# Two-layer decoder trunk: a second ordinary pair in three SwiGLUs, extra operands made later, and layer norm and rotation without GpSimd

## The chip, the cores and the metric

The kernel runs on one core of one Trainium2 chip. The metric is the device time of one execution in microseconds (us); lower is better. All data is 32 bits wide.

## The reference

For 512 tokens of width 1024, two layers run one after the other, and a final RMSNorm follows:

```
x = x + 0.5 * swiglu(rms_norm(x, g1), w_gate, w_up, w_down)     # d_ff = 2816
x = x + mixer(rms_norm(x, g2))
x = x + 0.5 * swiglu(rms_norm(x, g3), w_gate, w_up, w_down)
```

with `swiglu(x) = (silu(x @ w_gate) * (x @ w_up)) @ w_down`. So there are four SwiGLUs, two in each layer.

The mixer of layer 0 (the even one) projects its input to q, k and v of 8 heads of 64 and to the two halves u and v of a gMLP. Attention is block-sparse, which for 512 tokens is plain causal attention over at most two blocks of 256. The gMLP is

```
v = layer_norm(v.reshape(B, S, 8, 64), ln_g, ln_b)       # per group of 64 channels
mixed = einsum('gts,bnsgd->bntgd', tril(w_s), v) + b_s   # chunks of 128 tokens
return u * mixed
```

The mixer of layer 1 (the odd one) is a differential attention: 8 heads, two q/k maps of 64 per head, 128 values per head; the two softmaxes are subtracted with a weight lambda, and each head's output is normalised. In both, q and k are rotated by position in their first 16 of 64 dimensions: `x * cos + swap(x) * sin`.

## The kernel before

Everything stands transposed: `x[k]` for k = 0 to 7 holds 128 features by 512 tokens, in on-chip memory for the whole run. Weights stream from HBM in chunks of 128 x 1024. Each chunk is split into two fp32r parts: ScalarE copies it to `w_hi` (L120), VectorE subtracts to make `w_lo` (L121). A product is then three matmuls (`mm3`, L168 to L170): hi by hi, and the two cross terms. Activations are split in the same way (`xh`, `xl` in `Norm.split`, L217 and L218).

All work is issued as a list of slots (`Stream`). A slot names the chunks it needs and the function that issues its matmuls. `run` walks over the slots: `step()` first issues the side work that was put down for this slot by `later(n, fn)` ("n slots from now"), then the splits of chunks for later slots (four ahead in a SwiGLU, the next slot's in a mixer), then the slot's matmuls. A scheduler then orders each engine's instructions by the dependencies, by that order of issue and by its own estimates; each engine works in the resulting order.

A SwiGLU has 22 tiles of 128 features. Tile 0 and tile 11 are computed as ordinary products (`first`, `gate`, `up`, `product`), gate and up 8 x 3 matmuls with 512 columns each. The other tiles are taken in pairs (s, s + 11), and each pair, gate and up together, is computed by a Strassen-Winograd scheme with seven products instead of eight on halves of the tokens (`Step`, L424 to L426 in the profile: seven slots of 24 matmuls with 256 columns). That scheme needs sums of weights (partly made by a DMA that adds, L369, partly on VectorE, L380) and extra operands, which are sums of parts of x: `SevenNorm.sums_for(p)`, p = 0 to 3 makes them (three small splits and three sums, L281 to L290 and L264: seven operations on VectorE, five on ScalarE, each with 256 columns), and `last_sums` (L300, L301) a last one. The extra operands are made as soon as the x they need exist (`feed`: one slot after the k-th x), and for the first SwiGLU all four two slots after its first one.

The norm's factor for each token comes from squares summed over features (on GpSimd, L311, but for the first), a matmul with ones (`pc`, L240), ten small operations on VectorE (`rsqrt`, L191 to L202, result `rcol`), four transposes (`pr`, L322) and a copy on ScalarE (`R`, L326, also `norm.row`). It multiplies the SwiGLU's products after the matmuls (`product`), so TensorE can begin before it is known.

In the even mixer the gMLP's v is centred (`center`), scaled by its root (L840), multiplied by the gain and given the bias on GpSimd (L842, L843), and split one slot later (`split_gate`). In both mixers `rotated` makes a q or a k: VectorE swaps rows (L638) and multiplies by cosine (L639), GpSimd multiplies the swapped one by sine (L640) and adds the two (L641). Then ScalarE and VectorE split it (`qs`, L653 and L654; `ks`, L661 and L662). The heads' further stages (scores with exponentials `e`, transposes `pt`, their splits `ph` and `pl`, the product `o`) are put down some slots later.

Of the kernel before, what the change touches and what calls it, by code (L numbers as in the profile page):

```python
# [11 lines left out]
F32 = mybir.dt.float32  # L12
# [6 lines left out]
P = 128  # L19
# [13 lines left out]
def trunk_kernel(ctx: ExitStack, tc: tile.TileContext, a, out):  # L33
# [137 lines left out]

    warm = const.tile([P, 1], F32, name="warm")
    nc.vector.memset(warm, 0.0)
# [81 lines left out]
    class SevenNorm(Norm):  # L255
# [57 lines left out]
        def feed(self, k):  # L313
            self.split(k)
            self.square(k)
            if k in KHI:
                st.later(1, lambda: self.sums_for(KHI.index(k)))
# [30 lines left out]
    def ffn(which, norm, feed):  # L348
        gu, wd = a[f"gu{which}"], a[f"wd{which}"]
        H = {}  # L350

# [172 lines left out]
        def first(wg, wu):  # L524
            norm.finish_soon(1 + int(which == 0))
            pg, pu = bank("pg"), bank("pu")
            for ks in [[k] for k in range(KT)] if which == 0 else (range(KT - 1), range(KT - 1, KT)):
                for b, w in ((pg, wg), (pu, wu)):
                    project(b, w, norm, ks)
            for p in range(4):  # L530
                norm.whole(p)
            st.later(2 + int(which == 0), lambda: product(0, pg, pu))

        def gate(f):
# [5 lines left out]
        def up(f):  # L540
            def fn(w):
                b = bank("pu")
                project(b, w, norm)
                st.later(1, lambda: product(f, banks[f], b))
                st.later(1, norm.last_sums)
            return fn

        st.add([chunk(gu[0, 0]), chunk(gu[0, 1])], first, dense=True, raws=6)
        st.add([chunk(gu[HF, 0])], gate(HF), dense=True, raws=6)
        st.add([chunk(gu[HF, 1])], up(HF), dense=True, raws=6)  # L550
        add(1, 1)
        for s0, s1 in PARTS:
            for s in range(max(s0, 1), s1):
                for c in ORDER:
                    if c != 1:
                        add(s, c)
                    elif s + 1 < HF:
                        add(s + 1, 1)
            cols = slice(s0 * P, s1 * P)
            for ds in [(0, 1)] + [(d,) for d in range(2, KT)]:  # L560
                st.add([chunk(wd[0, d][:, cols], wd[1, d][:, cols]) for d in ds], down(ds, s0, s1),
                       dense=True, raws=6)
# [71 lines left out]
    def rotated(pq, tables, place):  # L634

        cr, sr = tables
        sw, q = tmp("sw"), tmp("q")
        nc.vector.stream_shuffle(sw, pq, SWAP)  # L638
        nc.vector.tensor_mul(q, pq, cr)  # L639
        nc.gpsimd.tensor_mul(sw, sw, sr)  # L640
        nc.gpsimd.tensor_add(q, q, sw)  # L641
        st.mids.append(lambda: place(q))
# [139 lines left out]
    def even_mixer(norm, feed):  # L782
# [9 lines left out]
        def begin():  # L792
            norm.finish_soon()
            st.later(3, lambda: box.update(rope=rope_tables(norm)))
            for c in range(2):
# [7 lines left out]
                wsl.append(lo)  # L803
            ln = act.tile([P, 2, T], F32, name="ln", tag="e", bufs=EB)
            for n, name in enumerate(("lng", "lnb")):
                box[name] = ln[:, n]
                nc.sync.dma_start(box[name], a["ln"][n])
            bs = act.tile([P, T], F32, name="bs", tag="e", bufs=EB)
            nc.sync.dma_start(bs, a["bs"])
            box["bs"] = bs.rearrange("p (m t) -> p m t", t=P)  # L810

# [24 lines left out]
        def finish_gate():  # L836
            rsqrt(rs.rearrange("p t g -> p (t g)"), s2.rearrange("p t g -> p (t g)"), 1.0 / 64, TT * 8)
            for t in range(TT):
                g = cen[t]
                nc.vector.tensor_tensor(by_group(g), by_group(g),  # L840
                                        rs[:, t, :, None].to_broadcast([P, 8, 64]), op=OP.mult)
                nc.gpsimd.tensor_mul(g, g, box["lng"])  # L842
                nc.gpsimd.tensor_add(g, g, box["lnb"])  # L843
            st.later(1, lambda: [split_gate(t) for t in range(TT)])

# [20 lines left out]
        def mix_group(m):  # L866
# [3 lines left out]
            for nn in range(2):  # L870
# [7 lines left out]
                for h in range(2):  # L878
                    r = slice(h * 64, h * 64 + 64)
                    nc.vector.tensor_tensor(mixv[r, 2 * nn:2 * nn + 2], bv[r, :, h],  # L880
                                            box["bs"][r, m:m + 1, :].to_broadcast([64, 2, P]), op=OP.add)
            nc.vector.tensor_mul(mix, mix, u[m])
# [56 lines left out]
    def odd_mixer(norm, feed):  # L939
# [71 lines left out]
        def values(p):  # L1011
            def fn(wa, wb):
                b = [bank("pv"), bank("pv")]
                for t in range(TT):
                    r = slice(t * P, (t + 1) * P)
                    for k in range(KT):
                        w = (wa, wb)[k // 4]
                        s = slice((k % 4) * 256, (k % 4 + 1) * 256)
                        mm3(b[t // 2][:, (t % 2) * 256:(t % 2 + 1) * 256], norm.hi[k][:, r], norm.lo[k][:, r],
                            w[0][:, s], w[1][:, s], k == 0, k == KT - 1)  # L1020
                halves = [t2k("h", "v", F32R).rearrange("p (n c) -> p n c", n=2) for _ in range(3)]
# [5 lines left out]
                box["v", p] = (vh, vl, vw)  # L1027
            st.add([chunk(a["ov"][p, 0]), chunk(a["ov"][p, 1])], fn)

# [167 lines left out]
```

## Time and profile before

| | |
|---|---|
| Median of three runs | 1886.41 us (1886.3 to 1890.41) |
| The profiled execution: time, span | 1890.68 us, 1888.9 us |
| Mean granted TensorE clock | 0.986 |
| TensorE (PE), matmul busy | 1834.6 us, 97% of the span |
| VectorE (DVE) busy | 1359.1 us, 72% |
| ScalarE (ACT) busy | 875.4 us, 46% |
| GpSimd (POOL) busy | 415.0 us, 22% |
| Mean HBM traffic | 127 GB/s |

The span is the time from the first to the last instruction; some 1.8 us of the execution lie outside it. The shares are means over stages that differ, so where an engine waits has to be read by stretch. The granted clock is a share of 2.4 GHz: 1.00 is full speed, 0.50 is 1.2 GHz.

### The profile page before, as it was taken

The page shows a single profiled execution, that of the slowest core. Times are in us where ns is not written, and L with a number is a line of the kernel's source. Part 1 is how long each engine was busy: PE and PEld are TensorE (multiplying, and loading weights), DVE is VectorE, ACT ScalarE, POOL GpSimd, SP SyncE. Part 2 cuts the span into 40 slices and gives each one's busy share as a digit, 9 for nine tenths or more (in the row PEclk, how much of TensorE's full clock was granted, in tenths as well). Part 3 has the DMA queues.
Part 4 walks back from the last instruction along what each step waited for, and adds up shares of the span by engine and source line. Part 5 has one row for each costly group of instructions (what it writes and reads, how often), then busy time and mean ns, then how long its engine had stood idle before and what let it go on. Part 6 is the DMA issues. An engine that isn't in the chain of part 4 may idle for free.

```text
span 1888.9 us, 29622 instructions
## 1 busy us (share of the span) xinstructions
PE 1834.6 (97%) x11612; PEld 1663.2 (88%) x11612; DVE 1359.1 (72%) x1949; ACT 875.4 (46%) x1302; POOL 415.0 (22%) x369
## 2 busy tenths in 40 slices
PE   7999999999898999999999999999899989999997
PEld 6989989878787989989899998988788779899896
DVE  8857748766758857748976685787798788578484
ACT  6524525433655524525554352544555455345252
POOL 1111011542522111010310111143433221110113
PEclk8999999999998999999999999999999999999999
DMA  7656656422334656656565565542232346566561
GB/s 201 176 141 154 168 122 168 129 66 69 90 97 94 177 141 152 168 124 156 134 152 154 129 178 135 149 135 67 90 90 90 95 95 169 144 157 163 124 160 45
DMA packets 197468, 247.74 MB, mean 131 GB/s; under 512 B 14272, under 2 KB 166480, under 8 KB 197328
## 3 DMA queue, kind: packets, MB, share of 16 engines
q1 hardware_dynamic: 153200, 202.81, 34.6%
q0 software_dynamic: 43552, 41.98, 15.1%
q8 instruction: 91, 1.49, 0.3%
q10 hardware_dynamic: 576, 1.05, 0.1%
q14 instruction: 49, 0.40, 0.1%
HBM read 237.40 MB, written 2.10 MB: 127 GB/s over the span
## 4 chain that ended last, share of the span: by engine, by line
PE 82%; DVE 7%; POOL 4%; ACT 3%; issue 2%; DMA 1%; SPq 0%; DVEq 0%; POOLq 0%; ACTq 0%
PE py L168 10%; PE py L170 10%; PE py L169 9%; PE pA L424 8%; PE pA L425 8%; PE pA L426 8%; PE pD L426 4%; PE pD L425 4%; PE pD L424 4%; PE pB L426 2%; PE pB L425 2%; PE pB L424 2%; POOL q L641 1%; DVE w_lo L121 1%; ACT e L690 1%
## 5 line engine op out<-in xcount | busy, mean ns | idle before, releaser
L120 ACT ACTIVATE w_hi<-w_raw 128x1024 fp32r<-128x1024 f32 (+1 forms) x450 | 467.8, 1042 | 619.7 <-PE py L169 210.9
L121 DVE TENSOR_TENSOR w_lo<-w_raw,w_hi 128x1024 fp32r<-128x1024 f32 (+1 forms) x450 | 558.5, 1242 | 178.6 <-ACT w_hi L120 144.3
L369 POOL DMA_DIRECT2D w_raw<-in_gu x160 | 173.6, 1209 | 985.2 <-DMA w_raw<-in_gu 522.4
L169 PE MATMUL py<-hl,w_hi 128*128 128x512 f32 x704 | 274.2, 389 | 0.0
L170 PE MATMUL py<-hh,w_lo 128*128 128x512 f32 x704 | 273.9, 389 | 0.0
L168 PE MATMUL py<-hh,w_hi 128*128 128x512 f32 x704 | 273.2, 390 | 0.0
L503 DVE SCALAR_TENSOR_TENSOR x<-py,x 128x512 f32<-128x512 f32 x96 | 66.0, 688 | 170.1 <-PE py L170 170.1
L424 PE MATMUL pA<-xh,w_hi 128*128 128x256 f32 x640 | 182.7, 285 | 0.0
L425 PE MATMUL pA<-xl,w_hi 128*128 128x256 f32 x640 | 182.1, 285 | 0.0
L426 PE MATMUL pA<-xh,w_lo 128*128 128x256 f32 x640 | 182.1, 285 | 0.0
L424 PE MATMUL pA<-xt,w_hi 128*128 128x256 f32 x640 | 181.2, 283 | 0.0
L426 PE MATMUL pA<-xt,w_lo 128*128 128x256 f32 x640 | 181.1, 283 | 0.0
L425 PE MATMUL pA<-xt,w_hi 128*128 128x256 f32 x640 | 181.1, 283 | 0.0
L169 PEld LDWEIGHTS py<-hl,w_hi 128*128 128x128 f32 x704 | 132.2, 188 | 27.6 <-DVE hl L482 0.8
L170 PEld LDWEIGHTS py<-hh,w_lo 128*128 128x128 f32 x704 | 132.2, 188 | 27.5
L168 PEld LDWEIGHTS py<-hh,w_hi 128*128 128x128 f32 x704 | 131.9, 188 | 27.8 <-ACT hh L477 1.2
L424 PEld LDWEIGHTS pA<-xh,w_hi 128*128 128x128 f32 x640 | 123.9, 194 | 1.5 <-ACT v L436 1.4
L425 PEld LDWEIGHTS pA<-xl,w_hi 128*128 128x128 f32 x640 | 123.9, 194 | 0.1
L426 PEld LDWEIGHTS pA<-xh,w_lo 128*128 128x128 f32 x640 | 123.9, 194 | 0.0
L424 PEld LDWEIGHTS pA<-xt,w_hi 128*128 128x128 f32 x640 | 122.9, 192 | 0.2 <-ACT v L436 0.2
L426 PEld LDWEIGHTS pA<-xt,w_lo 128*128 128x128 f32 x640 | 122.9, 192 | 0.0
L425 PEld LDWEIGHTS pA<-xt,w_hi 128*128 128x128 f32 x640 | 122.9, 192 | 0.0
(241 smaller groups left out, 4344.5 us busy)
## 6 DMA issues: line engine op xcount, KB each, us to landing
w_raw<-in_gu SPq DMA_DIRECT2D x402, 256.0 KB, 4.0
w_raw<-in_gu POOLq DMA_DIRECT2D x160, 256.0 KB, 5.3
w_raw<-in_wd SPq DMA_DIRECT2D x128, 256.0 KB, 3.0
w_raw<-in_wd SPq DMA_DIRECT2D x64, 192.0 KB, 2.5
w_raw<-in_oqk SPq DMA_DIRECT2D x16, 512.0 KB, 4.0
w_raw<-in_gu SPq DMA_DIRECT2D x14, 512.0 KB, 4.0
ks<-ks SPq DMA_DIRECT2D x24, 256.0 KB, 3.2
w_raw<-in_eqk SPq DMA_DIRECT2D x8, 512.0 KB, 3.7
```

What stands on the lines that cost most here:

```text
L120: nc.scalar.activation(hi, raw, AF.Copy)
L121: nc.vector.tensor_sub(lo, raw, hi.bitcast(F32))
L168: nc.tensor.matmul(o, sh, mh, start=first, stop=False)
L169: nc.tensor.matmul(o, sh, ml, start=False, stop=False)
L170: nc.tensor.matmul(o, sl, mh, start=False, stop=last)
L369: nc.gpsimd.dma_start(dst, src, accum_op=OP.add)
L424: nc.tensor.matmul(o, w[0][:, s], t[0], start=new and p + g == 0, stop=False, **go)
L425: nc.tensor.matmul(o, w[0][:, s], t[1], start=False, stop=False, **go)
L426: nc.tensor.matmul(o, w[1][:, s], t[0], start=False, stop=p == 3, **go)
L503: nc.vector.scalar_tensor_tensor(x[d], py[d], 0.5, x[d], op0=OP.mult, op1=OP.add)
L641: nc.gpsimd.tensor_add(q, q, sw)
L690: nc.scalar.activation(e, e, AF.Exp, bias=nm[:, i:i + 1], scale=-1.0, accum_out=su[:, o + i:o + i + 1])
```

## The change

Four things change.

1. In the SwiGLUs 0, 1 and 3 (those whose x comes from the input or from a mixer) a second pair of tiles, 1 and 12, is computed as an ordinary product ahead of the seven-product steps. There the extra operands are made in the four slots behind the first one, no longer as x arrives. SwiGLU 2, which follows SwiGLU 1, stays as it was.
2. Layer norm's gain and bias leave GpSimd. The gain is one number for a row of the transposed result, so it is multiplied in the operation that adds `b_s` (`mix_group`). The bias times the row sums of `w_s` is added to `b_s` ahead of time (`biases`: four matmuls with ones and eight small operations). `ln` becomes two loads of 4 numbers per partition.
3. The rotation's last two operations move from GpSimd to VectorE.
4. In the odd mixer, the slot that computes the values of two heads from two chunks becomes two slots with one chunk each, so the heads' stages are also counted in more slots.

```diff
@@ SevenNorm.feed
-            if k in KHI:
+            if k in KHI and self.early:
                 st.later(1, lambda: self.sums_for(KHI.index(k)))
@@ ffn
+        plain = 1 if which == 2 else 2
+        norm.early = plain == 1
...
             st.later(2 + int(which == 0), lambda: product(0, pg, pu))
+            if plain > 1:
+                for p in range(4):
+                    st.later(1 + p, lambda p=p: norm.sums_for(p))
...
-                st.later(1, lambda: product(f, banks[f], b))
-                st.later(1, norm.last_sums)
+                st.later(1 if norm.row else 2, lambda: product(f, banks[f], b))
+                if f == HF + plain - 1:
+                    st.later(1, norm.last_sums)
...
-        st.add([chunk(gu[HF, 0])], gate(HF), dense=True, raws=6)
-        st.add([chunk(gu[HF, 1])], up(HF), dense=True, raws=6)
-        add(1, 1)
+        for f in range(plain):
+            for f in (f, f + HF):
+                if f > 0:
+                    st.add([chunk(gu[f, 0])], gate(f), dense=True, raws=6)
+                    st.add([chunk(gu[f, 1])], up(f), dense=True, raws=6)
+        add(plain, 1)
         for s0, s1 in PARTS:
-            for s in range(max(s0, 1), s1):
+            for s in range(max(s0, plain), s1):
@@ rotated
-        nc.gpsimd.tensor_mul(sw, sw, sr)
-        nc.gpsimd.tensor_add(q, q, sw)
+        nc.vector.tensor_mul(sw, sw, sr)
+        nc.vector.tensor_add(q, q, sw)
@@ even_mixer, begin
-            ln = act.tile([P, 2, T], F32, name="ln", tag="e", bufs=EB)
-            for n, name in enumerate(("lng", "lnb")):
-                box[name] = ln[:, n]
-                nc.sync.dma_start(box[name], a["ln"][n])
+            ln = sm.tile([P, 2, 4], F32, name="ln", bufs=1)
+            for n in range(2):
+                nc.sync.dma_start(ln[:, n], a["ln"][n, 0:1].rearrange("o (m p) -> p (o m)", p=P))
...
+            def biases():
+
+                for c in range(2):
+                    b = bank("prow")
+                    nc.tensor.matmul(b, one, wsh[c], start=True, stop=False)
+                    nc.tensor.matmul(b, one, wsl[c], start=False, stop=True)
+                    for i in range(4):
+                        m, r = 2 * c + i // 2, slice(i % 2 * 64, i % 2 * 64 + 64)
+                        nc.vector.scalar_tensor_tensor(bs[r, m], b[r, i * P:(i + 1) * P], ln[r, 1, m:m + 1],
+                                                       bs[r, m], op0=OP.mult, op1=OP.add)
+            st.later(4, biases)
@@ finish_gate
-                nc.gpsimd.tensor_mul(g, g, box["lng"])
-                nc.gpsimd.tensor_add(g, g, box["lnb"])
-            st.later(1, lambda: [split_gate(t) for t in range(TT)])
+                split_gate(t)
@@ odd_mixer, values: one slot for each of two chunks
-            st.add([chunk(a["ov"][p, 0]), chunk(a["ov"][p, 1])], fn)
+            for n in range(2):
+                st.add([chunk(a["ov"][p, n])], half(n))
@@ end
-    for p in range(4):
-        st.later(2, lambda p=p: norms[0].sums_for(p))
```

What the scheduler makes of it is shown at three places. The first is VectorE at the start of SwiGLU 1, where the even mixer's output projection still delivers x (`x_70` to `x_77` are x[0] to x[7]). Before, between the fourth x and the next w_lo:

```order
L575 TENSOR_TENSOR x_74<-py,x_74 128x512
L284 SCALAR_TENSOR_TENSOR x_5397<-x_70,neg_gains,x_5396 128x256
L287 SCALAR_TENSOR_TENSOR xt_5399<-x_5396,neg_gains,xt_5399 128x256
L290 SCALAR_TENSOR_TENSOR x_5398<-x_72,neg_gains,x_5397 128x256
L264 TENSOR_TENSOR xt_5400<-x_5397,xt_5400 128x256
L264 TENSOR_TENSOR xt_5401<-x_5396,xt_5401 128x256
L282 TENSOR_TENSOR x_5413<-x_71 128x256
L283 SCALAR_TENSOR_TENSOR x_5413<-x_71,neg_gains,x_5414 128x256
L575 TENSOR_TENSOR x_75<-py,x_75 128x512
L284 SCALAR_TENSOR_TENSOR x_5414<-x_71,neg_gains,x_5413 128x256
```

In the changed kernel, from the fourth x to the first extra operand:

```order
L584 TENSOR_TENSOR x_74<-py,x_74 128x512
L218 SCALAR_TENSOR_TENSOR xl<-x_73,gains,xh 128x512
L584 TENSOR_TENSOR x_75<-py,x_75 128x512
L218 SCALAR_TENSOR_TENSOR xl<-x_74,gains,xh 128x512
L121 TENSOR_TENSOR w_lo<-w_raw,w_hi 128x1024
L218 SCALAR_TENSOR_TENSOR xl<-x_75,gains,xh 128x512
L121 TENSOR_TENSOR w_lo<-w_raw,w_hi 128x1024 x3
L584 TENSOR_TENSOR x_76<-py,x_76 128x512
L121 TENSOR_TENSOR w_lo<-w_raw,w_hi 128x1024
L218 SCALAR_TENSOR_TENSOR xl<-x_76,gains,xh 128x512
L584 TENSOR_TENSOR x_77<-py,x_77 128x512
L218 SCALAR_TENSOR_TENSOR xl<-x_77,gains,xh 128x512
```

The operations of the extra operands (L282 to L290, L264) have left this stretch; five splits of weights stand in it. On TensorE, a first matmul of pg stood before in the middle of the output projection's last matmuls (py), 20 of them behind it; now all of py stands ahead of pg.

The second place is ScalarE in SwiGLU 0, around the copy of R. Before:

```order
L120 ACTIVATE w_hi<-w_raw 128x1024
L300 ACTIVATE xh<-x_302 128x256
L120 ACTIVATE w_hi<-w_raw 128x1024 x3
L326 ACTIVATE R<-pr 128x512
L517 ACTIVATE gu<-gu 128x512
```

In the changed kernel:

```order
L285 ACTIVATE xt_454<-x_452,neg_gains 128x256
L263 ACTIVATE xt_455<-x_453 128x256
L326 ACTIVATE R<-pr 128x512
L120 ACTIVATE w_hi<-w_raw 128x1024
L263 ACTIVATE xt_456<-x_452 128x256
L519 ACTIVATE gu<-gu 128x512
```

Four w_hi stood ahead of R; now the first w_hi that the matmuls behind the transposes need stands behind it.

The third place is VectorE in the odd mixer, where the first head's probabilities (`e`) are combined and transposed. Before:

```order
L976 SCALAR_TENSOR_TENSOR e<-e,su_12949 128x384
L976 SCALAR_TENSOR_TENSOR e<-e,su_12949 128x512
L638 STREAM_SHUFFLE sw<-pq 128x512
L639 TENSOR_TENSOR q<-pq,rope 128x512
L121 TENSOR_TENSOR w_lo<-w_raw,w_hi 128x1024 x2
L715 TENSOR_TENSOR pl<-pt,ph 128x512
```

In the changed kernel:

```order
L999 SCALAR_TENSOR_TENSOR e<-e,su_12712 128x384
L999 SCALAR_TENSOR_TENSOR e<-e,su_12712 128x512
L663 TENSOR_TENSOR qs<-q,qs 64x512
L648 TENSOR_TENSOR q<-pq,rope 128x512
L649 TENSOR_TENSOR sw<-sw,rope 128x512
L724 TENSOR_TENSOR pl<-pt,ph 128x512
L650 TENSOR_TENSOR q<-q,sw 128x512
```

The two w_lo ahead of pl are gone; the rotation's sine product (L649) stands there, its sum (L650) behind the first pl.

## Rows read from the trace of the kernel before

**Rows 1.** Windows: us, busy us (instructions) of each engine, granted clock, DMA share, GB/s.
```profile
60.00:340.00 280.00, 280.00 (x1951) 262.58 (x1951) 193.10 (x215) 123.92 (x150) 35.86 (x33) 1.00 0.60 153
```

**Rows 2.** Windows, TensorE alone: us, busy us (matmuls), granted clock, DMA share, GB/s.
```profile
28.00:48.00 20.00, 13.67 (x79) 0.74 0.38 72
404.00:424.00 20.00, 16.43 (x62) 0.91 0.28 91
482.00:522.00 40.00, 33.24 (x158) 0.91 0.28 79
568.00:588.00 20.00, 14.64 (x50) 0.74 0.29 56
1334.00:1350.00 16.00, 9.42 (x47) 0.79 0.49 157
1508.00:1530.00 22.00, 15.37 (x54) 0.84 0.28 58
```

**Rows 3.** Waits of TensorE: us in total, times, longest us.
```profile
PE pg L168 <- ACT w_hi L120: 10.0, 2, 5.1
PE o L169 <- DVE pl L715: 6.6, 1, 6.6
```

**Rows 4.** Timeline of TensorE, two dense runs: start us, us, then the instruction.
```profile
98.83 0.28 PE L424 MATMUL pA<-xh,w_hi 128*128 128x256 f32 x1
...
103.99 0.28 PE L425 MATMUL pD<-xl,w_hi 128*128 128x256 f32 x1
...
339.51 0.39 PE L168 MATMUL py<-hh,w_hi 128*128 128x512 f32 x1
...
352.21 0.39 PE L170 MATMUL py<-hh,w_lo 128*128 128x512 f32 x1
```

**Rows 5.** Timeline of SwiGLU 0's start; idle time and its releaser in brackets.
```profile
20.68 0.16 DVE L191 TENSOR_SCALAR rs<-pc 128x4 f32<-128x4 f32 x1 [0.32 <-PE pc L240]
...
37.22 0.16 DVE L202 SCALAR_TENSOR_TENSOR rcol<-rs,rs 128x4 f32<-128x4 f32 x1
...
36.95 2.00 ACT L120 ACTIVATE w_hi<-w_raw 128x1024 fp32r<-128x1024 f32 x2 [2.90 <-DVE w_raw L380]
38.85 0.58 ACT L326 ACTIVATE R<-pr 128x512 f32<-128x512 f32 x1
...
37.52 1.08 PE L322 MATMUL pr<-ident,rcol 128*128 128x128 f32 x4 [6.33 <-DVE rcol L202]
```

**Rows 6.** Timeline of layer norm, ScalarE and VectorE.
```profile
406.32 0.63 ACT L333 ACTIVATE gh<-gv 128x512 fp32r<-128x512 f32 x1 [7.08 <-POOL gv L843]
...
408.47 2.28 DVE L121 TENSOR_TENSOR w_lo<-w_raw,w_hi 128x1024 fp32r<-128x1024 f32 x1
```

**Rows 7.** Groups by line: instructions, busy us, mean ns, idle us before them.
```profile
L641 POOL TENSOR_TENSOR q<-q,sw 128x512 f32<-128x512 f32 x24 | 37.0, 1542 | 1.6
L640 POOL TENSOR_TENSOR sw<-sw,rope 128x512 f32<-128x512 f32 x24 | 32.5, 1354 | 86.7 <-DVE sw L638 86.6
L639 DVE TENSOR_TENSOR q<-pq,rope 128x512 f32<-128x512 f32 x24 | 16.3, 681 | 4.4 <-POOL rope L625 4.2
```

**Rows 8.** Timeline of ScalarE in the even attention.
```profile
508.13 0.63 ACT L661 ACTIVATE ks<-q 64x512 fp32r<-64x512 f32 x1 [3.76 <-POOL q L641]
```

**Rows 9.** Timeline of VectorE in the odd attention.
```profile
1339.02 4.14 DVE L121 TENSOR_TENSOR w_lo<-w_raw,w_hi 128x1024 fp32r<-128x1024 f32 x2
```

**Rows 10.** Timeline of SwiGLU 1's start, GpSimd and VectorE.
```profile
561.81 5.41 POOL L311 TENSOR_TENSOR acc<-acc,sq 128x512 f32<-128x512 f32 x3 [13.93 <-ACT sq L309]
...
562.04 2.33 DVE L121 TENSOR_TENSOR w_lo<-w_raw,w_hi 128x1024 fp32r<-128x1024 f32 x1
...
575.55 1.21 DVE L121 TENSOR_TENSOR w_lo<-w_raw,w_hi 128x1024 fp32r<-128x1024 f32 x1
```

**Rows 11.** Windows of the two attentions, VectorE alone: us, busy us (instructions).
```profile
1290.00:1500.00 210.00, 170.11 (x405) 0.98 0.29 88
465.00:525.00 60.00, 43.95 (x103) 0.94 0.33 96
```

More of the change, by code (lines that the diff above doesn't have):

```diff
@@ L170, in mm3 @@
         nc.tensor.matmul(o, sl, mh, start=False, stop=last)
-    warm = const.tile([P, 1], F32, name="warm")
+    warm = tmp("warm")[:, :1]
     nc.vector.memset(warm, 0.0)
@@ L803, in begin @@
                 wsl.append(lo)
-            ln = act.tile([P, 2, T], F32, name="ln", tag="e", bufs=EB)
-            for n, name in enumerate(("lng", "lnb")):
-                box[name] = ln[:, n]
-                nc.sync.dma_start(box[name], a["ln"][n])
+            ln = sm.tile([P, 2, 4], F32, name="ln", bufs=1)
+            for n in range(2):
+                nc.sync.dma_start(ln[:, n], a["ln"][n, 0:1].rearrange("o (m p) -> p (o m)", p=P))
+            box["ln"] = ln
             bs = act.tile([P, T], F32, name="bs", tag="e", bufs=EB)
             nc.sync.dma_start(bs, a["bs"])
-            box["bs"] = bs.rearrange("p (m t) -> p m t", t=P)
+            box["bs"] = bs = bs.rearrange("p (m t) -> p m t", t=P)
+            one = t2k("r2", "ones", F32R)[:, :P]
+            nc.vector.tensor_copy(one, ones1.to_broadcast([P, P]))
+            def biases():
[8 more added lines that the diff above has]
+            st.later(4, biases)
         def by_group(g):
@@ L879, in mix_group @@
                     r = slice(h * 64, h * 64 + 64)
-                    nc.vector.tensor_tensor(mixv[r, 2 * nn:2 * nn + 2], bv[r, :, h],
-                                            box["bs"][r, m:m + 1, :].to_broadcast([64, 2, P]), op=OP.add)
+                    nc.vector.scalar_tensor_tensor(mixv[r, 2 * nn:2 * nn + 2], bv[r, :, h],
+                                                   box["ln"][r, 0, m:m + 1],
+                                                   box["bs"][r, m:m + 1, :].to_broadcast([64, 2, P]),
+                                                   op0=OP.mult, op1=OP.add)
             nc.vector.tensor_mul(mix, mix, u[m])
@@ L1011, in values, with half, fn, evac @@
         def values(p):
[L1012 to L1020, printed above, removed]
+            b = []
+            def half(n):
+                def fn(w):
+                    if n == 0:
+                        b.extend(bank("pv") for _ in range(2))
+                    for t in range(TT):
+                        r = slice(t * P, (t + 1) * P)
+                        o = b[t // 2][:, (t % 2) * 256:(t % 2 + 1) * 256]
+                        for k in range(4 * n, 4 * n + 4):
+                            s = slice((k % 4) * 256, (k % 4 + 1) * 256)
+                            go = {"skip_group_check": True}
+                            nc.tensor.matmul(o, norm.hi[k][:, r], w[0][:, s], start=k == 0 and t % 2 == 0,
+                                             stop=False, **go)
+                            nc.tensor.matmul(o, norm.hi[k][:, r], w[1][:, s], start=False, stop=False, **go)
+                            nc.tensor.matmul(o, norm.lo[k][:, r], w[0][:, s], start=False, stop=k == KT - 1, **go)
+                    if n == 1:
+                        evac()
+                return fn
+            def evac():
                 halves = [t2k("h", "v", F32R).rearrange("p (n c) -> p n c", n=2) for _ in range(3)]
```

## The prediction

> **What bounds the kernel now.** I read the windows first. In the stretch from 60 to 340 us [rows 1] TensorE is busy for all of its time at full clock; the same holds for three more such stretches (600 to 900, 945 to 1230, 1530 to 1840 us), so the inside of each SwiGLU is bound by TensorE alone and nothing that another engine saves there is worth anything. What can be won lies in a few short places. [rows 2] are the six that I found by following TensorE's waits [rows 3]; they are called here A (first SwiGLU's start), B (layer norm), C (the even attention), E (the odd attention), D and F (the starts of the second and the fourth SwiGLU). The reader sees two losses in each row: idle time, and a clock granted below 1.00, which follows each wait (two levels, 1.2 and 2.4 GHz). I take as a place's loss the window minus its busy time, plus the busy time times what is missing from the clock: A 6.3 + 13.7 x 0.26 = 9.9 us, B 3.6 + 1.5 = 5.0, C 6.8 + 3.0 = 9.8, D 5.4 + 3.8 = 9.2, E 6.6 + 2.0 = 8.6, F 6.6 + 2.5 = 9.1. Together 51.6 us of the profiled 1890.7: more than that can't come from stalls there.
>
> **The change, part by part.**
>
> *Work added to TensorE.* A pair of ordinary feature tiles is 4 x 8 x 3 = 96 matmuls with 512 columns; by seven products it is 7 x 24 = 168 with 256. In [rows 4] the starts of a dense run are 56 steps apart in 12.70 us for 512 columns, so 0.227 us each, and 43 steps in 5.16 us for 256, so 0.120. 96 x 0.227 - 168 x 0.120 = 1.63 us more for a pair. Three SwiGLUs get such a pair: 4.9 us. The bias terms are 4 matmuls with 512 columns, 0.9 us. Sum: +5.8 us, on the engine that is the bound, so it counts in full.
>
> *A, start of the first SwiGLU.* The ten small steps of the norm's root stand between [rows 5] 20.68 and 37.22 us on VectorE, mixed with all four sets of extra operands and with splits of weights; TensorE stood 6.33 us for its result. In the new order two sets stand between them (each seven operations of 256 columns, some 2.7 us at 0.33 to 0.40 a step), one split of 1.2 us and the ten steps of about 0.1: some 8 us, so the result comes near 29 us, ahead of TensorE, which gets there at about 31.2. What is late next is the order on ScalarE: the copy of R now stands ahead of the second pair's first w_hi. TensorE does the transposes (1.08), R takes 0.58, w_hi 1.0 (two took 2.00), all in [rows 5], and w_lo 1.2 behind two products of 0.68: I take 3 us of waiting and a little lost clock, 3.5 us left of 9.9. Bounds: 1 us if these overlap, 6.5 if w_lo comes behind all sums.
>
> *B, layer norm.* ScalarE idles 7.08 us [rows 6] for GpSimd's gain and bias, and the weights' w_hi is queued behind that copy; VectorE's w_lo beside GpSimd takes 2.28 us. Both steps on GpSimd go; the split follows VectorE's product at once. New on VectorE: eight short bias operations ahead of the means (bounded by 0.68 each [rows 7], an operation on eight times the elements: at most 5.4 us; I take 2, since ScalarE's 7 us of slack cover the rest). Left: 1.5 us (0.5 to 4).
>
> *C and E, the rotations.* On GpSimd the two operations take 1.35 + 1.54 us [rows 7], and ScalarE waits for them with the scores' exponentials behind it (3.76 us in [rows 8]); on VectorE they cost 2 x 0.68, or 2 x 0.6 from start to start. So each q or k comes about 1.5 us earlier, and VectorE gets 24 x 2 x 0.6 = 29 us more work. Part of that comes back: [rows 9] show two w_lo in 4.14 us beside GpSimd's rotation; 2 x 1.2 is what they take otherwise. The Trainium skill (SBUF — State Buffer, Who interferes with whom) says that a VectorE instruction with two SBUF inputs and a GpSimd one that reads SBUF exclude each other for a whole instruction. That agrees with the row; by the rule alone the change would free up to all 69.5 us of GpSimd's rotations for VectorE, whereas the sum goes by rows. In E, besides, w_lo of both value chunks stood ahead of the pl for which TensorE waited 6.6 us [rows 3]; with half the chunk in a slot, pl stands ahead of any w_lo, behind one operation of qs and two of the rotation, some 2.5 us instead of 5.4. Left: C 5 us (2 to 9.8), E 4 us (1.5 to 8.6); the upper ends are no gain at all, the lower ones a third of the chain that remains through ScalarE.
>
> *D and F, starts of the second and the fourth SwiGLU.* TensorE waits 10.0 us in two waits for w_hi of pg [rows 3]; ScalarE waits there for VectorE, which makes two sets of extra operands (13 to 14 operations, about 5.5 us, more beside GpSimd's sum of squares: a w_lo took 2.33 instead of 1.21 [rows 10]) ahead of them. Now no set stands ahead of the splits, and the rest of the output projection's matmuls stands ahead of pg, so they cover the wait that is left. The sets come later: three of them (some 8 to 11 us) ahead of the norm's root. TensorE needs that root only after three passes of 24 x 0.227 = 5.4 us behind the last x, so 16 us; the two ordinary pairs, which take 43 us and need no extra operand, cover the fourth. If that cover were gone, the wait of A would come back here (about 5 us each). Left: D 1.5 us (0.5 to 4), F 2 us (0.5 to 5).
>
> *At nothing:* the gain in layer norm moves into an operation that is there already; `warm` and `ln` move to other memory; the two small loads of `ln` stand ahead of one weight chunk on SP's queue in the first microseconds, and a late chunk would be a wait inside A's range; products a step later (A) hold PSUM banks, of which six of eight are in use. Less splitting in an ordinary pair (4 w_lo instead of 7, no sums of weights) frees VectorE inside the SwiGLU, where TensorE never waits.
>
> **Sum.** Left 3.5 + 1.5 + 5 + 1.5 + 4 + 2 = 17.5 of 51.6, so 34.1 us won; 5.8 us lost; net 28.3. The profiled execution took 1890.7 us, the median is 1886.4 and the lowest 1886.3; the places are the same in all, so I take the difference off the median: 1858 us.
>
> **The rivals.**
>
> *1. VectorE becomes the bound in the mixers: 1867 us.* It is busy 170 of 210 us in the odd one and 44 of 60 around C [rows 11]. C's 60 us hold only 50 of undisturbed TensorE work, and 44 + 5 x 1.2 less 5 x 0.87 of relief (half of 4.14 - 2.4 for each rotation) is 45.7: nearly full. The Trainium skill (Perfetto Trace Analysis, Optimizing Scalar/DVE Operations) advises the reverse of this change for a saturated VectorE: offload to ScalarE or even GpSimd. If it binds, C and E keep their loss (18.4 instead of 9): 1858 + 9.4 = 1867. Against it: in the odd mixer 170 + 16 x (1.2 - 0.87) is 175 of about 200.
>
> *2. The waits all but vanish: 1847 us.* With every lower bound 6 us stay: 45.6 - 5.8 = 39.8 off. For it speaks that each place has one named cause; against it, that each removed wait has the next one close behind (R, pl, the root).
>
> *3. The starts' waits only move: 1879 us.* The sets of extra operands are as many as before. If the root comes late by the time that the splits now gain, A, D and F keep 28.2 us: 3.5 + 4.8 + 4.6 - 5.8 = 7.1 off. Against it, 16 us for 11 of work.
>
> *4. Slower: 1900 us.* One mechanism: VectorE's 48 new operations stand on the chain of the mixers one by one, 48 x 0.68 = 33 us, with A, B, D and F won (24.7) and 5.8 paid: +14. It decides from the point at which VectorE has no idle time in the mixers; 175 of 200 us speaks against it.
>
> **How the numbers follow.** Forecast 0.62, rival 1 0.18, rival 2 0.10, rival 3 0.07, rival 4 0.03. The likeliest gives 1858. Its own bounds, with half of the places at either end, are about 1848 and 1868; rivals 1 and 2 lie next to them. The range 1843 to 1873 takes them in and leaves out rivals 3 and 4 and some of the tails. A measurement of this kernel tells 0.3%, 5.7 us, from no change: faster than 1880.7 are the forecast, rivals 1 and 2 and half of 3, 0.93; same 0.045 (the rest of 3, a little of 1); slower 0.025.
>
> **What would show it.** The 256-column products fall by 504 and the 512-column matmuls rise by 292. TensorE's wait for rcol in A falls from 6.3 to under 1, and one of 2 to 3 us for w_hi follows. No wait for w_hi of pg over 1 us at D and F, and at most one stretch of half clock in both. No GpSimd operation between 385 and 560 us but squares, tables and e. C and E keep 9 us of waits, for pl, ph and ml. The prediction is wrong if VectorE is busy over 95% in the mixers with TensorE waiting for q, if a wait for rcol of several us stands at D or F, or if the long dense stretches show idle time.

## The result and the profile after

The changed kernel takes 1868.38 us (median of four runs, 1865.04 to 1869.47), the kernel before 1886.88 us (four runs). The ratio is 0.9892 with a 95% interval of 0.9877 to 0.9907: 18.5 us won at the medians, where the prediction said 28.3. The profiled executions differ by 1890.68 - 1869.47 = 21.2 us.

The page of the changed kernel, busy time of each engine: us, share of the span, instructions.

```profile
PE 1831.7 (98%) x11400; PEld 1653.1 (89%) x11400; DVE 1349.9 (72%) x1985; ACT 861.0 (46%) x1284; POOL 323.4 (17%) x301
```

TensorE has 212 matmuls fewer than before (11612), which is the forecast's 292 more of 512 columns and 504 fewer of 256. VectorE's share is still 72%, although the rotation came to it.

The windows that answer to [rows 1] and [rows 2], TensorE alone. The columns are those of [rows 2].

```profile
28.00:48.00 20.00, 17.59 (x72) 0.91 0.62 142
400.00:420.00 20.00, 16.97 (x67) 0.91 0.35 105
475.00:515.00 40.00, 39.25 (x211) 1.00 0.35 100
545.00:565.00 20.00, 17.53 (x69) 0.91 0.22 63
1340.00:1360.00 20.00, 15.83 (x86) 0.83 0.20 65
1486.00:1506.00 20.00, 16.00 (x70) 1.00 0.24 69
1515.00:1530.00 15.00, 13.95 (x68) 1.00 0.70 155
60.00:340.00 280.00, 280.00 (x1936) 1.00 0.58 148
```

Taken as in the prediction (idle time plus busy time times the missing clock), A keeps 2.4 + 1.6 = 4.0 us, B 3.0 + 1.5 = 4.6, C 0.8, D 2.5 + 1.6 = 4.1, E 4.2 + 2.7 = 6.9, F 4.0 + 1.1 = 5.1 (two windows). Together 25.5 us of the 51.6 of before, where 17.5 were forecast. 26.1 won and 5.8 paid give 20.3, close to the 21.2 of the two profiles. So the budget closes to within a microsecond; what has to be explained is the size at each place.

TensorE's waits in the changed kernel: us in total, times, longest.

```profile
PE py L170 <- DVE w_lo L121: 6.5, 4, 2.5
PE pr L322 <- DVE ocol L202: 4.4, 2, 4.2
PE pv L169 <- DVE w_lo L121: 1.7, 1, 1.7
PE pg L168 <- ACT w_hi L120: 1.6, 1, 1.6
PE pr L322 <- DVE rcol L202: 1.4, 2, 1.1
PE pv L168 <- ACT w_hi L120: 1.3, 1, 1.3
PE o L169 <- DVE pl L724: 0.2, 1, 0.2
```

The three long waits of before (pr for rcol in A, pg for w_hi, o for pl [rows 3, 5]) are gone or short. Two that were short before stand in their place: the output projections' own matmuls (py) wait for w_lo at D and F (2.0 us in all before), and in E the transposes of a head's root (pr) wait for `ocol` (1.1 us before). The timeline of E shows how the second comes about: start us, us, engine and instruction, idle time and releaser in brackets.

```profile
1347.16 0.15 DVE L191 TENSOR_SCALAR rs<-pc 128x4 f32<-128x4 f32 x1
...
1349.17 0.69 DVE L697 CUSTOM_DVE_ANT_0 e<-s,mask 128x512 f32<-128x512 f32 x1
...
1349.85 1.22 DVE L121 TENSOR_TENSOR w_lo<-w_raw,w_hi 128x1024 fp32r<-128x1024 f32 x1
...
1351.07 0.72 DVE L647 STREAM_SHUFFLE sw<-pq 128x512 f32<-128x512 f32 x1
1351.68 0.15 DVE L199 SCALAR_TENSOR_TENSOR rs<-rs,rs 128x4 f32<-128x4 f32 x1
...
1352.42 0.69 DVE L649 TENSOR_TENSOR sw<-sw,rope 128x512 f32<-128x512 f32 x1
...
1353.14 0.69 DVE L650 TENSOR_TENSOR q<-q,sw 128x512 f32<-128x512 f32 x1
1353.75 0.16 DVE L202 SCALAR_TENSOR_TENSOR ocol<-rs,rs 128x4 f32<-128x4 f32 x1
1353.96 1.11 PE L322 MATMUL pr<-ident,ocol 128*128 128x128 f32 x4 [4.17 <-DVE ocol L202]
```

The ten steps need 1.5 us of work, but from the first to the last 6.7 us pass, because VectorE takes them in turn with the mask, a split and the rotation's four operations.

### The profile page after: what moved, and what is told of

The parts are those of the page before. It is cut to its first block, busy times and chain, and to the rows that moved or that the text cites. A ratio compares the mean times of both kernels' runs of the same rounds, so it can differ in the third digit from the quotient of the medians.

```text
span 1867.7 us, 29044 instructions
## 1 busy us (share of the span) xinstructions
PE 1831.7 (98%) x11400; PEld 1653.1 (89%) x11400; DVE 1349.9 (72%) x1985; ACT 861.0 (46%) x1284; POOL 323.4 (17%) x301
## 4 chain that ended last, share of the span: by engine, by line
PE 62%; DVE 6%; ACT 1%; issue 1%; DMA 0%; POOL 0%; DVEq 0%; POOLq 0%; ACTq 0%
PE py L168 7%; PE py L169 7%; PE py L170 7%; PE pA L426 6%; PE pA L427 6%; PE pA L428 6%; PE pD L428 3%; PE pD L426 3%; PE pD L427 3%; PE pB L426 1%; PE pB L428 1%; PE pB L427 1%; DVE w_lo L121 1%; PE pq L168 1%; PE pq L170 1%; PE pq L169 1%
## 5 line engine op out<-in xcount | busy, mean ns | idle before, releaser
L121 DVE TENSOR_TENSOR w_lo<-w_raw,w_hi 128x1024 fp32r<-128x1024 f32 (+1 forms) x441 | 540.9, 1227 | 167.8 <-ACT w_hi L120 130.0
L371 POOL DMA_DIRECT2D w_raw<-in_gu x148 | 160.7, 1200 | 994.3 <-DMA w_raw<-in_gu 545.9
L426 PE MATMUL pA<-xh,w_hi 128*128 128x256 f32 x592 | 168.2, 284 | 0.0
L428 PE MATMUL pA<-xt,w_lo 128*128 128x256 f32 x592 | 167.8, 283 | 0.0
L427 PE MATMUL pA<-xt,w_hi 128*128 128x256 f32 x592 | 167.8, 283 | 0.0
L428 PE MATMUL pA<-xh,w_lo 128*128 128x256 f32 x592 | 167.8, 283 | 0.0
L426 PE MATMUL pA<-xt,w_hi 128*128 128x256 f32 x592 | 167.8, 283 | 0.0
L427 PE MATMUL pA<-xl,w_hi 128*128 128x256 f32 x592 | 167.8, 283 | 0.0
L168 PEld LDWEIGHTS py<-hh,w_hi 128*128 128x128 f32 x704 | 132.0, 188 | 28.3 <-ACT hh L479 1.5
L426 PEld LDWEIGHTS pA<-xh,w_hi 128*128 128x128 f32 x592 | 113.7, 192 | 1.5 <-ACT v L438 1.4
L427 PEld LDWEIGHTS pA<-xl,w_hi 128*128 128x128 f32 x592 | 113.7, 192 | 0.2
L426 PEld LDWEIGHTS pA<-xt,w_hi 128*128 128x128 f32 x592 | 113.8, 192 | 0.0
L427 PEld LDWEIGHTS pA<-xt,w_hi 128*128 128x128 f32 x592 | 113.8, 192 | 0.0
```

The source lines that it names most:

```text
L121: nc.vector.tensor_sub(lo, raw, hi.bitcast(F32))
L168: nc.tensor.matmul(o, sh, mh, start=first, stop=False)
L371: nc.gpsimd.dma_start(dst, src, accum_op=OP.add)
L426: nc.tensor.matmul(o, w[0][:, s], t[0], start=new and p + g == 0, stop=False, **go)
L427: nc.tensor.matmul(o, w[0][:, s], t[1], start=False, stop=False, **go)
L428: nc.tensor.matmul(o, w[1][:, s], t[0], start=False, stop=p == 3, **go)
```

## The experiments

Twelve kernels were run, each beside the kernel before on the same chip, so ratios to before are compared.

**The four parts taken back one at a time.** The edits are the hunks of the change, reversed: SwiGLU pairs, layer norm, rotation, value slots.

```diff
-        plain = 1 if which == 2 else 2
+        plain = 1
...
```


> The changed kernel with part 1 taken back: one ordinary pair in every SwiGLU, the extra operands made as x arrives, four sets two slots behind the first in SwiGLU 0. Theory 1 (the sizes of the prediction): A, D and F lose 6.4 + 7.7 + 7.1 us again, 4.9 us of matmuls go: 16.3 us over the 1868 us of the changed kernel, 1884 us. Theory 2 (the sizes in the changed kernel's trace, where D and F keep waits that were not foreseen, because the output projection's own last matmuls now wait for w_lo): A 4.9, D 4, F 5.7, less 4.9, so 9.7 us: 1878 us.

1875.61 us, ratio 0.9938 (0.9924 to 0.9951). Pairs and late operands are worth 7.2 us net, under both expectations. The waits of [rows 3, 5] come back (pr for rcol 6.3, pg for w_hi 10.3 in two), but py's wait for w_lo falls from 6.5 to 2.9: 3.6 us of the wait at D and F had only moved.

```diff
-                split_gate(t)
+                nc.gpsimd.tensor_mul(g, g, box["lng"])
+                nc.gpsimd.tensor_add(g, g, box["lnb"])
+            st.later(1, lambda: [split_gate(t) for t in range(TT)])
...
```


> The changed kernel with part 2 taken back: gain and bias of layer norm on GpSimd, the split a slot later, no bias matmuls. Theory 1 (prediction): B loses 3.5 us again and 0.9 us of matmuls go, 1871 us. Theory 2: B's wait only moved (5.25 us of loss in the changed kernel, 6.3 before), so the two cancel: 1868 us, within 1 us of the changed kernel.

1869.39 us, 0.9905 (0.9892 to 0.9919): no difference that can be told, theory 2. The changed kernel's timeline of B shows what took the place of GpSimd's wait:

```profile
402.36 0.19 DVE L202 SCALAR_TENSOR_TENSOR ln_rs<-rs,rs 128x32 f32<-128x32 f32 x1
...
403.37 1.83 ACT L333 ACTIVATE gh<-gv 128x512 fp32r<-128x512 f32 x3 [3.69 <-DVE gv L863]
...
405.10 1.04 ACT L120 ACTIVATE w_hi<-w_raw 128x1024 fp32r<-128x1024 f32 x1
...
406.20 0.73 PE L168 MATMUL pv<-w_hi,xh 128*128 128x512 f32 x2 [1.29 <-ACT w_hi L120]
...
407.40 1.22 DVE L121 TENSOR_TENSOR w_lo<-w_raw,w_hi 128x1024 fp32r<-128x1024 f32 x1
...
408.67 0.50 PE L169 MATMUL pv<-w_lo,xh 128*128 128x512 f32 x1 [1.74 <-DVE w_lo L121]
```

ScalarE's idle time fell from 7.08 us [rows 6] to 3.69, but now three copies gh (1.83 us) stand ahead of the w_hi that TensorE needs, and gl, gv and u ahead of its w_lo. The root of layer norm itself is late: it is ready only at 402.5 us.

```diff
-        nc.vector.tensor_mul(sw, sw, sr)
-        nc.vector.tensor_add(q, q, sw)
+        nc.gpsimd.tensor_mul(sw, sw, sr)
+        nc.gpsimd.tensor_add(q, q, sw)
```


> The changed kernel with part 3 taken back: sine product and sum of the rotation on GpSimd. Theory 1 (prediction): C loses 4.8 us again and E some 2: 1875 us. Theory 2 (the trace of the changed kernel: C's loss fell by 10 us, while in E the ten steps of a head's root now stand between the rotation's four operations on VectorE and TensorE waits 4.2 us for them): C loses 10 us again, E wins back 3 to 6 of its 6.6: 1872 to 1875 us, and the wait for ocol in E is gone. Rival 1 of the prediction (VectorE binds in the mixers) would make this kernel faster than the changed one, under 1868 us.

1887.04 us, 0.9998 (0.9989 to 1.0007). Neither expectation: without the two lines nothing is left of the gain, 18.7 us instead of 4 to 7. Where TensorE loses them is seen in windows that hold the same number of matmuls in both kernels, around C and around the odd mixer and the start of its projection (us, busy us (matmuls), clock, DMA share, GB/s). The rotation on GpSimd:

```profile
459.53:556.30 96.77, 90.89 (x452) 0.95 0.29 88
1272.39:1489.36 216.97, 207.65 (x1203) 0.97 0.28 85
```

The changed kernel:

```profile
460.64:547.09 86.45, 85.70 (x452) 1.00 0.33 97
1263.61:1471.50 207.89, 202.93 (x1203) 0.98 0.30 89
```

The first is 10.3 us longer, the second 9.1, together more than the 17.5 us between the two profiled spans: the whole loss lies at the two attentions, as idle time and as half clock.

```diff
-            for n in range(2):
-                st.add([chunk(a["ov"][p, n])], half(n))
+            st.add([chunk(a["ov"][p, 0]), chunk(a["ov"][p, 1])], fn)
...
```


> The changed kernel with part 4 taken back: one slot for the values of two heads. Theory 1 (prediction): w_lo of both chunks stand ahead of pl again, E loses 2.5 to 4.6 us: 1871 to 1873 us, with a wait of o for pl of some 5 us. Theory 2: the wait for ocol is what E keeps, it belongs to the new count of slots and goes with it, and the wait for pl takes its place: 1868 to 1870 us.

1863.66 us, 0.9873 (0.9860 to 0.9887): 4.7 us faster than the changed kernel at the medians, though the intervals overlap, and neither expectation in time. Theory 2's mechanism is there: in its trace the odd mixer waits once for pl, and not for ocol at all; the next fences show the wait and the window of the odd mixer (all five engines: us, busy us of PE, PEld, DVE, ACT, POOL).

```profile
PE o L169 <- DVE pl L724: 2.7, 1, 2.7
```
```profile
1257.00:1438.00 181.00, 178.01 (x1077) 158.55 (x1076) 161.21 (x374) 97.11 (x214) 24.60 (x33) 1.00 0.29 87
```

**Do rotation and slots interact?**

```diff
-        nc.vector.tensor_mul(sw, sw, sr)
-        nc.vector.tensor_add(q, q, sw)
+        nc.gpsimd.tensor_mul(sw, sw, sr)
+        nc.gpsimd.tensor_add(q, q, sw)
...
-            for n in range(2):
-                st.add([chunk(a["ov"][p, n])], half(n))
+            st.add([chunk(a["ov"][p, 0]), chunk(a["ov"][p, 1])], fn)
...
```


> Parts 3 and 4 taken back together; pairs and layer norm stay changed. Alone, taking back the rotation cost 18.7 us and taking back the value slots won 4.7. Theory 1 (the parts add up): 1868.4 + 18.7 - 4.7 = 1882 us. Theory 2 (the two interact: with a value chunk in a slot of its own the heads' stages come at other moments, and with the rotation on GpSimd these meet w_lo and the root's steps at four places of the odd mixer; with the old slots only the one wait of o for pl comes back, some 8.5 us, and C's 10): 1868.4 + 10 = 1878 us or less, with one long wait of o for pl in E and no waits for v or ocol.

1882.21 us, 0.9966 (0.9954 to 0.9978). These two parts add up within the noise (the medians' differences sum to 1882.4). The new slots cost 4.8 us with the rotation on GpSimd as well (1887.04 against 1882.21, and there the intervals are apart), the rotation is worth 18.6 us with the old slots. By the ratios the slots cost 3.6 and 6.0 us and the rotation is worth 20.0 and 17.5, so none of these figures holds to the microsecond.

**The rotation alone.**

```diff
@@ before, rotated
-        nc.gpsimd.tensor_mul(sw, sw, sr)
-        nc.gpsimd.tensor_add(q, q, sw)
+        nc.vector.tensor_mul(sw, sw, sr)
+        nc.vector.tensor_add(q, q, sw)
```


> The kernel before with part 3 alone: the rotation's last two operations on VectorE, two lines. Theory 1 (the parts add up, and the rotation carries the whole gain: 18.7 us with the new value slots, 18.5 with the old): 1887.0 - 18.6 = 1868.4 us, the same as the whole change, ratio 0.990. Theory 2 (the prediction's sizes: C 4.8 us and some 2 of E): 1880 us. Theory 3 (rival 1: without the relief of the other parts VectorE binds in the mixers): 1884 us or more.

1873.27 us, 0.9919 (0.9905 to 0.9932): 14.4 us from two lines, most of the whole change's gain, some 4 us less at the medians than adding up would have it. The profiled spans differ by 17.3 us (1888.9 and 1871.6), as with the other two pairs of kernels that differ in the rotation alone (17.5 and 17.1), so the missing 4 us are not clear of the noise. o's wait for pl falls from 6.6 [rows 3] to 2.7 us with the old slots. What changes ahead of TensorE's waits is seen on ScalarE: its waits for the finished q or k, which stand ahead of everything else in its queue. Before,

```profile
ACT qs L653 <- POOL q L641: 43.8, 12, 7.7
ACT ks L661 <- POOL q L641: 31.3, 11, 5.5
```

in the changed kernel,

```profile
ACT ks L670 <- DVE q L650: 25.1, 9, 6.1
ACT qs L662 <- DVE q L650: 21.9, 9, 4.8
```

and in the changed kernel with the rotation on GpSimd:

```profile
ACT ks L670 <- POOL q L650: 39.6, 11, 6.3
ACT qs L662 <- POOL q L650: 31.4, 11, 5.5
```

75.1, 47.0 and 71.0 us in total: ScalarE stands 24 to 28 us less for q (in the changed kernel it stands another 5.3 us ahead of one ks, for which the profile shows no releaser). That these waits are what TensorE lost is argued from the queue, not shown by a run. The two mixers' windows, changed kernel, engines as above:

```profile
436.00:496.00 60.00, 59.29 (x302) 50.51 (x301) 56.05 (x116) 32.73 (x68) 14.42 (x14) 1.00 0.31 88
1258.00:1445.00 187.00, 182.13 (x1093) 163.02 (x1092) 165.19 (x394) 100.06 (x223) 27.44 (x38) 0.98 0.29 84
```

VectorE is busy 56 of 60 us around C, and TensorE all the same for 59.3 of them at full clock.

**GpSimd's load without its place in the chain.**

```diff
         nc.vector.tensor_add(q, q, sw)
+        nc.gpsimd.tensor_mul(sw, q, sr)
+        nc.gpsimd.tensor_add(sw, sw, q)
```


> The changed kernel, with two further operations on GpSimd behind each rotation, of the size of those that left it: q times the sine table into the tile of the swapped rows, and q added to it. Nothing reads that tile afterwards, so only GpSimd's load and what it does to its neighbours come back, not the place in q's chain. Theory 1 (the rotation's gain is the shorter chain: no hop to GpSimd and back ahead of the splits): 1868 us, at most 1871. Theory 2 (the gain is that GpSimd no longer slows VectorE's neighbours, w_lo 1.22 instead of 1.33 us and ks 0.68 instead of 0.81 on the mean): these means rise again and most of the 18.7 us is lost, 1880 us or more. GpSimd's scaling of e, which now stands behind these operations in its queue, is part of theory 2's loss.

1892.71 us, 1.0019 (1.0011 to 1.0028): 24 us over the changed kernel and over before too. Theory 2 by the time. Two groups of VectorE, the changed kernel (instructions, busy us, mean ns):

```profile
L663 DVE TENSOR_TENSOR qs<-q,qs 64x512 fp32r<-64x512 f32 x24 | 16.6, 693 | 0.7
L671 DVE TENSOR_TENSOR ks<-q,ks 64x512 fp32r<-64x512 f32 x24 | 16.4, 685 | 3.8 <-ACT ks L670 3.5
```

and the one with the two operations more:

```profile
L673 DVE TENSOR_TENSOR ks<-q,ks 64x512 fp32r<-64x512 f32 x24 | 25.8, 1075 | 3.8 <-ACT ks L672 3.3
L665 DVE TENSOR_TENSOR qs<-q,qs 64x512 fp32r<-64x512 f32 x24 | 25.4, 1058 | 0.7
```

The splits beside the additional GpSimd work take 1.06 to 1.08 us instead of 0.69: 18.2 us more of VectorE, and the odd mixer's waits for ocol grow from 4.4 to 13.7 us. In the longest of these, 5.6 us, even small steps of the root stretch, to 1.23 and 1.08 us from the 0.16 that they take elsewhere:

```profile
1452.41 1.23 DVE L195 TENSOR_TENSOR rs<-rs 128x4 f32<-128x4 f32 x1
```

VectorE has no new wait for the tiles that GpSimd now holds longer. The means of w_lo did not move as theory 2 had it (1.232 against 1.227 us over the whole kernel); what collides is what VectorE does next, above all the splits of q. ScalarE's waits for q grew with it, from 47.0 to 64.3 us, so a shorter chain alone didn't keep them short. This is not the kernel before: there the same splits took only 0.78 and 0.77 us on the mean. So the run shows that GpSimd's work beside these splits is dear; it doesn't say which share of the 18.7 us is collision and which the shorter chain. GpSimd's scaling of e, queued behind the additional operations, made TensorE's transposes wait 2.5 us; that is part of it too.

**E's new wait.**

```diff
-                st.later(n, fn)
+                st.later(n + (fn is r and h < 6), fn)
```


> The changed kernel, but in the odd mixer the transposes of a head's root are put down one slot later (heads 0 to 5), so that nothing of the arithmetic changes. Theory 1 (E's loss of 6.6 us in the changed kernel is the wait of these transposes for the ten root steps, which VectorE works off between the rotation's operations, the mask's and a w_lo): that wait goes and with it its stretch of half clock, 1862 us. Theory 2 (VectorE is full in that place, so the next operation waits instead, o for pl or the scores for q): E keeps its loss, 1868 us.

1866.65 us, 0.9885 (0.9871 to 0.9898), which can't be told from the changed kernel. Its trace shows no wait for ocol any more; o waits for pl 1.6 us and py for pl 0.7 us, and the windows of the odd mixer and its projection have these losses:

```profile
1257.00:1441.00 184.00, 182.07 (x1096) 0.99 0.29 87
1441.00:1502.00 61.00, 56.37 (x269) 0.97 0.27 85
```

The named wait went (theory 1), and part of it was given back in the projection behind (a clock of 0.97 in the second window, where the changed kernel has 1.00). Taking the slots back has the lower median (1863.66), but the intervals overlap.

**The waits of py at D and F.** The timeline of the changed kernel at D:

```profile
555.11 1.71 DVE L218 SCALAR_TENSOR_TENSOR xl<-x,gains,xh 128x512 fp32r<-128x512 f32 x1
...
556.60 1.34 POOL L311 TENSOR_TENSOR acc<-acc,sq 128x512 f32<-128x512 f32 x1 [0.34 <-ACT sq L309]
556.73 2.29 DVE L121 TENSOR_TENSOR w_lo<-w_raw,w_hi 128x1024 fp32r<-128x1024 f32 x1
...
559.08 0.50 PE L170 MATMUL py<-mh,w_lo 128*128 128x512 f32 x1 [2.10 <-DVE w_lo L121]
```

The last chunk's w_lo stands behind an xl on VectorE, and both are slow beside GpSimd's additions of squares. Two kernels separate order and collision.

```diff
-                (nc.vector if by_act else nc.gpsimd).tensor_add(self.acc, self.acc, sq)
+                (nc.vector if by_act or self.idx in (2, 5) else nc.gpsimd).tensor_add(self.acc, self.acc, sq)
```


> The changed kernel, but in SwiGLU 1 and 3 the squares are added on VectorE instead of GpSimd (seven additions each). Theory 1 (the waits of the output projection for w_lo at D and F, 2.1 to 2.7 us each with a stretch of half clock, come from VectorE's operations beside GpSimd's additions: xl 1.7 instead of 0.7 us, w_lo 2.3 instead of 1.2): these operations return to their short durations, some 4 us in each place, against 7 x 0.6 = 4.2 us of additions, of which four or five stand behind the last w_lo of the projection; the waits fall below 1 us and 3 to 5 us are won: 1864 us. Theory 2 (it is the order alone, w_lo stands behind xl on VectorE): the additions only lengthen that queue, 1868 to 1872 us.

1866.40 us, 0.9888 (0.9875 to 0.9902): no difference that can be told. The durations went back (w_lo 1.22, xl 0.74 us), but the additions took their room, and py still waits 5.5 us for w_lo, the longest 3.5. Theory 2's mechanism, without its loss.

```diff
@@ run, slots that are not dense; on the kernel with the old value slots
-                        self.split_to(self.slots[i + 1][1])
+                        self.split_to(self.slots[min(i + 1 + (raws == 6), len(self.slots) - 1)][1])
```


> The changed kernel without part 4 (1863.7 us), and in the last four slots of each output projection the weights are split one slot earlier, so that w_lo stands ahead of one more xl on VectorE. Theory 1 (the waits of py for w_lo at D and F, 2.3 and 2.4 us and a stretch of half clock at D, come from that order): both go, 4 to 6 us, 1858 to 1860 us. Theory 2 (VectorE is full there, beside GpSimd's additions of squares, and the wait goes to xl, xh or the next w_lo): 1862 to 1864 us.

1865.64 us, 0.9877 (0.9864 to 0.9891), not distinguishable from the 1863.66 us without the edit. Its waits at D and F:

```profile
PE pr L322 <- DVE rcol L202: 6.1, 2, 3.2
...
PE py L170 <- DVE w_lo L121: 1.2, 2, 0.8
```

py's wait falls from 5.5 to 1.2 us, and TensorE comes earlier to the transposes of the norm's root (by 4.4 us at D, by 1.1 at F), where it now waits 3 us each for rcol. Theory 2 with another place: not xl but the root is late next. Here the prediction's rival 3 is seen at work.

**Is the second pair needed?**

```diff
-        plain = 1 if which == 2 else 2
-        norm.early = plain == 1
+        plain = 1
+        norm.early = which == 2
...
-            if plain > 1:
+            if not norm.early:
...
-                    st.later(1 + p, lambda p=p: norm.sums_for(p))
+                    st.later(1 + min(p, 2), lambda p=p: norm.sums_for(p))
```


> Part 1 without its second pair: in SwiGLU 0, 1 and 3 one ordinary pair, but the extra operands made in the three slots behind the first one. Theory 1 (prediction: the second pair is the cover for the root and the fourth set, and without it waits of some 5 us come back at D and F, and R's place at A): the 4.9 us of matmuls go, 5 to 15 us of waits come back, 1868 to 1878 us. Theory 2 (only the lateness of the operands matters, the second pair is nothing but work): 1868.4 - 4.9 = 1863.5 us, with a loss in the starts as in the changed kernel.

1866.57 us, 0.9887 (0.9874 to 0.9901): between the two theories. The wait for rcol at D and F grows from 1.4 to 4.2 us (theory 1), against 4.9 us of matmuls saved; the 1.8 us won at the medians are not clear of the noise. So the pair is cover, at about the price of what it covers, and what part 1 wins comes from making the extra operands later: apart from one product put down a slot later, that is all that separates this kernel from the 1875.61 us with early ones, and there the intervals are apart.

> As the kernel with old value slots and earlier splits, but with one ordinary pair in every SwiGLU, the operands made late. Theory 1 (the second pair pays with waits as much as it costs in matmuls, as in the changed kernel, where one pair took 1.8 us less): within 2 us of that kernel. Theory 2 (the pair covers the root and with earlier splits TensorE comes there sooner, so the wait for the root grows): 3 us or more over it.

The edit is that of the run before, on the kernel with old slots and earlier splits. 1866.93 us, 0.9888 (0.9872 to 0.9903), 1.3 us over that kernel: theory 1, though the wait for rcol does grow as theory 2 has it, from 6.1 to 9.1 us.

## Why the prediction was right in sum and wrong in its parts

The time fell into the range, on its upper side; the forecast was 10 us too good. That it fell there is in part luck: the rotation won 18.7 us where the prediction's terms give about 7, and this made up for the pairs, the layer norm and the slots. With 7 us for the rotation the time would have been 1880 us, outside the range. Of the signs named, those at A, D and F came in the main (no wait for rcol in A, none for w_hi of pg at D and F, one stretch of half clock there), and the 9 us left at C and E came to 7.7, but for ocol and not for pl, ph and ml. By its steps:

- **TensorE's +5.8 us**: the count of matmuls came out as worked out, and the long stretches stay at full clock without idle time.
- **A (3.5 forecast, 4.0 left)**: right, with its reason. pg waits 1.6 us for the w_hi behind R and 0.8 for w_lo, and no wait for rcol stands there; the rest, 1.6 us, is clock.
- **D and F (1.5 and 2 forecast, 4.1 and 5.1 left)**: the step that failed is "the rest of the output projection's matmuls stands ahead of pg, so they cover the wait that is left". The cover needed cover itself: its own last w_lo stands on VectorE behind xl, beside GpSimd's additions, and py waits for it; where that wait was taken away, the root of the norm was late by 3 us next, which 16 us for 11 of work was to exclude. The lower price of the pairs follows: 7.2 us net by the run without them, where the terms of A, D and F less 4.9 us gave 16.3.
- **B (1.5 forecast, 4.6 left)**: the step that failed is that the weights' splits follow once GpSimd is gone. The three gh and gl stand ahead of them and wait for the root. Layer norm's part can't be told from nothing.
- **C (5 forecast, 0.8 left)**: mis-sized the other way. I kept half of the loss for the chain through ScalarE; taking GpSimd out of it left next to nothing.
- **E (4 forecast, 6.9 left)**: two mistakes that partly cancel. "pl stands ahead of any w_lo" came true (o waits 0.2 us), but the rotation alone had brought that wait to 2.7, so the slots were not needed for it; and with them the root's ten steps fall among the rotation's operations, 4.2 us and a stretch of half clock. Part 4 was counted as a gain and costs some 4.7 us.
- **The share of the rotation**: about 7 us by the prediction's terms, 18.7 by the run without it and 14.4 by the run with it alone. The prediction took 1.5 us for each q or k and the one wait of [rows 8], kept half of C's loss, and gave E's wait for pl [rows 3] to the slots. The runs give the rotation nearly all of C's loss and most of E's. It left out that ScalarE stood 75.1 us in all for q, with splits, exponentials and copies behind it in its queue; that this is the reason is argued.

**Rival 1** (VectorE binds) was held for the likeliest alternative. It came nearest in the even mixer: VectorE is busy 56 of 60 us in the attention and 53.9 in the stretch from 460 to 520 us that answers to C's in [rows 11], more than the 45.7 I had worked out. The two operations are busy 17.9 + 17.3 us in the whole kernel, 0.75 and 0.72 us each where 0.68 was taken (the 29 us count from start to start), and the relief was smaller than 0.87 us for each rotation: at most 13.1 us for 24 rotations, the 6.5 and 6.6 named below. TensorE lost next to nothing there all the same (0.7 of 60 us). The Trainium skill (Perfetto Trace Analysis, Optimizing Scalar/DVE Operations) names GpSimd as a place to offload a saturated VectorE to, and adds that moving work between these two might not help; the run without the rotation's move agrees with the second half, by 18.7 us. **Rival 3** (the starts' waits only move) holds for about half of D and F. On the other rule cited from the Trainium skill, that a VectorE instruction with two SBUF inputs and a GpSimd one that reads SBUF exclude each other (SBUF — State Buffer, Who interferes with whom), the run with the additional GpSimd operations agrees in kind: 0.69 us became 1.06. That all 69.5 us come free is not shown; VectorE's e, qs and ks took 6.5 us less, w_lo 6.6 us less (441 by 15 ns), layer norm's part included.

**What stays open**: how the rotation's gain divides between the shorter wait of ScalarE and fewer collisions on VectorE, and whether the rotation alone really gives less (14.4 us) than with the other parts (18.6). The four parts taken back one at a time sum to 22.2 us (7.2 + 1.0 + 18.7 - 4.7), the whole change gives 18.5; what makes the difference is not shown. The fastest kernel measured is the change without its value slots, 1863.66 us; its interval overlaps that of the whole change, so the 4.7 us rest on the pair of runs with the rotation on GpSimd, whose intervals are apart, and on the missing wait for ocol.

## What to carry to other kernels

For a step that is offloaded in the middle of a chain, look beyond its own durations at the time that the next engine's queue stands for it; here a view of ScalarE's waits, grouped by releaser, would have shown 75 us. That is a warning and not a price: 24 to 28 us of it went, and some 18 us of time. The better measure stood in the prediction's own rows, TensorE's losses at C and E (18.4 us), of which it kept half. When work is put ahead as cover, ask what that work itself still waits for. And take parts of a change back one at a time: here one of four carried 18.7 us, one 7.2, one did nothing that can be told, and one cost some 4.7.

## What the runs showed that was not expected

Two operations on GpSimd that no result needs (1.38 and 1.57 us each, 24 times) made the kernel 24 us slower. In its trace the two-input splits on VectorE that stand beside them take 1.06 us instead of 0.69, and a step on 4 columns took 1.23 instead of 0.16. And VectorE at 93% busy in a 60 us stretch (56.05 us) let TensorE run through it at full clock.
